# Gates, projections and merge of a hybrid decoder block, by token instead of by feature

## The chip, the cores and the metric

The kernel runs on one core of a Trainium2 chip. The metric is the device time of one execution in microseconds (us); the median of several runs is compared. All times below come from those runs or from one profiled execution of the kernel before.

## The reference, cut to what matters

256 tokens, model width 2048, float32. The change touches the gated merge of two token mixers:

```python
u = rms_norm(h, g_mix)
proj = u @ w_in                       # (256, 8704)
q, k, v, z, gb, gc, gate_a, gate_c = jnp.split(proj, split_points, axis=-1)
...
y_attn = sliding_window_attention(q, k, v, attn_sinks) @ w_attn_proj     # K = 1024
y_conv = short_gated_conv(z, gb, gc, conv_w) @ w_conv_proj               # K = 1024
merged = sigmoid(gate_a) * y_attn + sigmoid(gate_c) * y_conv             # (256, 2048)
h = h + merged @ w_mix_out                                               # K = 2048
```

Cross attention to 256 memory tokens and a SwiGLU block follow, and are not changed.

## The kernel before, in words

**Products.** Every product takes its float32 weights from DRAM in tiles of 256 rows (two k of 128) by 512 columns (`weights`, L72). SP issues the load of `raw` (5 buffers). ScalarE (ACT) rounds it to `whi` (L57), VectorE (DVE) makes the rest `wlo` (L58); each of these has 3 buffers. The activations are kept as a high and a low part too. TensorE (PE) then has two forms of product:

- `gemm_ft` (L88) gives the result by feature: weights are the stationary operand, 128 features at a time, and four such groups fill four accumulators in PSUM (of 5). For each k and group it issues one matmul of 512 columns (`whi` against high and low activations side by side, L98) and one of 256 (`wlo` against the high part, L102): 8 matmuls for each k, 3072 columns. At the end each group costs an ACT copy of half the accumulator (L109) and what `evac` yields; the first step runs at once, the rest is put into `pending` and is taken up between the weight tiles of the next product (L78).
- `gemm_tf` (L114) gives it by token: the activations of 128 tokens are stationary, the 512 weight columns move. For each k and each of two token blocks it issues three matmuls of 512 columns (L124, L125, L126): 6 for each k, 3072 columns, in two accumulators. `evac` runs once for each token block.

**Order of the work.** One loop after another: q, k, v (`gemm_tf`), six conv products, then the gates (L544, 8 products of 16 k: four fill `sa`, four fill `sc`), then for each 512-column chunk c the attention projection (L593, 8 k) and the conv projection (L594, 8 k), then W_mix_out (L638, four products of 16 k that read the merged features `MG`). "Hooks" are small pieces of other work issued ahead of a given weight tile: attention during the gates, and during the projections (`mem_hooks`, L582) the loads, squares and turning of the memory tokens. A planner then writes each engine's queue: it simulates the program, takes the work traced first among what it believes ready, and so can move work ahead. `keep_in_program_order` (L216) keeps the first turning instruction of a pair behind what was traced before it on its engine; the second one is free to move. Each queue then runs strictly in its order.

**Around the change.** `evac_g` (L554) adds the halves, scales by the norm's factor and takes the sigmoid: two DVE and two ACT instructions for each group. `evac_a` (L566) multiplies the attention projection by its gate into `sa`; `evac_m` (L573) multiplies the conv projection by its gate, adds `sa` and splits the sum into `MG`: by feature is what W_mix_out needs as its stationary operand. Token-major data can be turned in two ways that exist here already: by a bounce through DRAM (`bounce_out` L235 writes `hd`, `bounce_in` L240 reads it back in four transfers, `feat` L207 turns 32x32 blocks on DVE with L214 and splits), as the SwiGLU stage does through POOL's queue (L819), or by TensorE transposes into PSUM (`h_turn`, L728).

Of the kernel before, what the change touches and what calls it, by code (L numbers as in the profile page):

```python
# [10 lines left out]
F32 = mybir.dt.float32  # L11
# [6 lines left out]
P = 128  # L18
D = 2048
# [22 lines left out]
def hybrid_block(ctx, tc, a, out):  # L42
# [220 lines left out]
    with ExitStack() as ph:  # L263
# [72 lines left out]

        sa = mp.tile([P, KD, T], F32, tag="sa", name="sa")


        def rotary(s_sb, nh):  # L340
            for t in range(NT):
              for h0 in range(0, nh, 8):
# [4 lines left out]
                sn = rope[:, t:t + 1, 1, :].broadcast_to([P, n8, HD // 2])  # L347
                tm = [sa[:, i, :].rearrange("p (h d) -> p h d", d=HD // 2)[:, :n8, :] for i in range(4)]
                tt = nc.gpsimd.tensor_tensor
# [155 lines left out]

        sc = mp.tile([P, KD, T], F32, tag="sc", name="sc")
        steps = {
# [36 lines left out]
        for dst, base in ((sa, AW + 2 * KVW + 3 * CW), (sc, AW + 2 * KVW + 3 * CW + D)):  # L544
            for c in range(D // C):
                hooks = {4 * j + 2: [f] for j, f in enumerate(steps.get(i, ()))}
                i += 1
                if i == 8:
                    mem_open()
                    do = mem_do  # L550
                    hooks = {0: [lambda: do["stage"](0)], 2: [lambda: do["stage"](1)],
                             4: [lambda: do["nat"](0)], 6: [lambda: do["nat"](1)]}

                def evac_g(m, p0, p1, c=c, dst=dst):  # L554
                    o = dst[:, c * (C // P) + m, :]
                    add(o, p0, p1)
                    yield
                    scale(o, r0[1])
                    nc.scalar.activation(o, o, AF.Sigmoid)

                gemm_ft(W, KD, X1, base + c * C, evac_g, hooks=hooks)


        MG = xp.tile([P, KD, 2, T], F32R, tag="X", name="MG")
        for c in range(D // C):
            def evac_a(m, p0, p1, c=c):  # L566
                mm = c * (C // P) + m
                s = sp.tile([P, T], F32, tag="s1", name="s1", bufs=4)
                add(s, p0, p1)
                yield  # L570
                nc.vector.tensor_tensor(out=sa[:, mm, :], in0=s, in1=sa[:, mm, :], op=ALU.mult)

            def evac_m(m, p0, p1, c=c):  # L573
                mm = c * (C // P) + m
                s = sp.tile([P, T], F32, tag="s1", name="s1", bufs=4)
                add(s, p0, p1)
                yield
                nc.vector.tensor_tensor(out=s, in0=s, in1=sc[:, mm, :], op=ALU.mult)
                nc.vector.tensor_tensor(out=s, in0=s, in1=sa[:, mm, :], op=ALU.add)
                split(MG[:, mm, 0, :], MG[:, mm, 1, :], s)  # L580

            def mem_hooks(g):  # L582
# [3 lines left out]
                if g < 4:  # L586
                    hk[2].append(lambda: do["turn"](g, 0))
                    hk[4].append(lambda: do["turn"](g, 2))
                    if g < 2:
                        hk[4].append(lambda: do["stage"](g + 2))  # L590
                return hk

            gemm_ft(rows_kp(a["w_attn_proj"][0]), AW // P, oT, c * C, evac_a, hooks=mem_hooks(2 * c))  # L593
            gemm_ft(rows_kp(a["w_conv_proj"][0]), KC, yc, c * C, evac_m, hooks=mem_hooks(2 * c + 1))  # L594
        while pending:
            next(pending.pop(0), None)
        ms.close()
# [16 lines left out]
    with ExitStack() as ph:  # L614
# [20 lines left out]
        def h_feat(c, k, g, X):  # L635
            feat(hs[c], C // P, k, 2, c * (C // P) + k, g, X)

        for c in range(D // C):  # L638
            hooks = {4: [lambda: nc.gpsimd.dma_start(h[:, :, c * C:(c + 1) * C], xv[:, :, c * C:(c + 1) * C])]}
            if c:  # L640
                hooks[4].append(lambda: h_stage(c - 1))
            if c == D // C - 1:
                hooks[4].append(mem_rms)
            gemm_tf(rows_kp(a["w_mix_out"][0]), KD, MG, c * C, residual(c, ss1), hooks=hooks)

# [213 lines left out]
```

## Time and profile before

| | |
|---|---|
| median of 3 runs | 1441.95 us (1441.08 to 1443.12) |
| profiled execution, its own time | 1436.75 us |
| its span, first to last instruction | 1434.9 us |
| TensorE busy | 1418.9 us (99%) |
| VectorE, ScalarE, GpSimd busy | 858.8, 691.1, 95.0 us |

How to read it: PE is TensorE's matmuls, PEld its weight loads, DVE VectorE, ACT ScalarE, POOL GpSimd, SP the queue of weight loads. L12 is line 12 of the kernel. A row of the timeline gives start, length, engine, line, operation, out<-in, shapes and count; in square brackets the idle time of the engine before it and what ended it. The lengths of neighbouring matmuls overlap, so rates are read from start to start. The profiled execution was 5.2 us shorter than the median; differences are worked out in it and carried to the median.

### The profile page before, as it was taken

What the parts mean: (1) busy time and instruction counts of PE and PEld (TensorE: products, weight loads), DVE (VectorE), ACT (ScalarE), POOL (GpSimd) and SP (SyncE); (2) the same over time, 40 slices, a digit from 0 to 9 for tenths busy, and PEclk for the clock granted to TensorE, in tenths of its full rate; (3) what the DMA queues carried; (4) which work ended last, traced back from release to release, by engine and by line L of the source; (5) the groups of instructions that cost most, each with busy time, mean ns of one, the idle gap of its engine ahead of it and who ended that gap; (6) DMA issues with size and microseconds to landing.
All of it is one profiled execution on the core that took longest, in us unless ns stands there. A gap on an engine that the chain in (4) does not pass through costs nothing.

```text
span 1434.9 us, 18603 instructions
## 1 busy us (share of the span) xinstructions
PE 1418.9 (99%) x7006; PEld 1190.6 (83%) x7006; DVE 858.8 (60%) x1162; ACT 691.1 (48%) x979; POOL 95.0 (7%) x145
## 2 busy tenths in 40 slices
PE   9999999999999999999999999999999999999997
PEld 7888888888888888899888888888888888888886
DVE  5458678565569865585655555555444455555554
ACT  6443545554456654466644444444333444434443
POOL 1081000010001010000000000000000000000000
PEclk9999999999999999999999999999999999999999
DMA  8665454476667677764667777767666677777663
GB/s 269 192 176 172 138 171 150 150 219 203 190 199 216 204 248 235 249 201 150 207 187 223 221 221 219 214 211 221 193 192 194 203 215 221 220 211 230 204 191 118
DMA packets 150186, 288.66 MB, mean 201 GB/s; under 512 B 10084, under 2 KB 18880, under 8 KB 149968
## 3 DMA queue, kind: packets, MB, share of 16 engines
q1 hardware_dynamic: 144192, 269.52, 61.7%
q0 software_dynamic: 5872, 17.94, 4.7%
q8 instruction: 55, 0.90, 0.3%
q14 instruction: 35, 0.29, 0.1%
q10 hardware_dynamic: 32, 0.01, 0.0%
HBM read 277.47 MB, written 9.96 MB: 200 GB/s over the span
## 4 chain that ended last, share of the span: by engine, by line
PE 95%; POOL 2%; DMA 1%; ACT 1%; issue 1%; DVE 0%; SPq 0%; ACTq 0%; POOLq 0%; DVEq 0%
PE acc L125 21%; PE acc L124 21%; PE acc L126 21%; PE acc L98 20%; PE acc L102 10%; PE sps L445 1%; PE ops L498 1%; PE tp L487 0%; POOL sa L351 0%; POOL sa L350 0%; DMA hd<-h 0%; DMA x<-in_x 0%; DMA hst<-hd 0%; POOL sa L353 0%; PE tp L733 0%
## 5 line engine op out<-in xcount | busy, mean ns | idle before, releaser
L58 DVE TENSOR_TENSOR wlo<-raw,whi 128x1024 fp32r<-128x1024 f32 (+1 forms) x506 | 607.8, 1206 | 501.9 <-ACT whi L57 501.6
L57 ACT CAST whi<-raw 128x1024 fp32r<-128x1024 f32 (+1 forms) x506 | 520.2, 1031 | 651.3 <-PE acc L126 448.1
L98 PE MATMUL acc<-X,whi 128*128 128x512 f32 x960 | 329.2, 397 | 0.0
L125 PE MATMUL acc<-wlo,X 128*128 128x512 f32 x800 | 311.2, 390 | 0.0
L126 PE MATMUL acc<-whi,X 128*128 128x512 f32 x800 | 310.5, 389 | 0.0
L124 PE MATMUL acc<-whi,X 128*128 128x512 f32 x800 | 280.2, 390 | 1.8 <-ACT X L227 1.8
L102 PE MATMUL acc<-X,wlo 128*128 128x256 f32 x960 | 247.8, 281 | 0.0
L98 PEld LDWEIGHTS acc<-X,whi 128*128 128x128 f32 x960 | 176.7, 188 | 35.2 <-issue 0.8
L102 PEld LDWEIGHTS acc<-X,wlo 128*128 128x128 f32 x960 | 180.7, 188 | 11.0 <-issue 0.8
L124 PEld LDWEIGHTS acc<-whi,X 128*128 128x128 f32 x800 | 149.8, 188 | 33.4 <-ACT X L227 2.6
L126 PEld LDWEIGHTS acc<-whi,X 128*128 128x128 f32 x800 | 150.1, 188 | 31.1
L125 PEld LDWEIGHTS acc<-wlo,X 128*128 128x128 f32 x800 | 150.2, 188 | 30.9
L125 PE MATMUL acc<-wlo,gT 128*128 128x512 f32 x352 | 137.0, 389 | 0.0
L126 PE MATMUL acc<-whi,gT 128*128 128x512 f32 x352 | 136.9, 389 | 0.0
L124 PE MATMUL acc<-whi,gT 128*128 128x512 f32 x352 | 123.1, 389 | 0.0
L125 PEld LDWEIGHTS acc<-wlo,gT 128*128 128x128 f32 x352 | 66.1, 188 | 14.0 <-DVE wlo L58 0.3
L124 PEld LDWEIGHTS acc<-whi,gT 128*128 128x128 f32 x352 | 66.1, 188 | 13.8
L126 PEld LDWEIGHTS acc<-whi,gT 128*128 128x128 f32 x352 | 66.1, 188 | 13.6
L125 PE MATMUL acc<-wlo,MG 128*128 128x512 f32 x128 | 49.9, 390 | 0.4 <-DVE wlo L58 0.4
L126 PE MATMUL acc<-whi,MG 128*128 128x512 f32 x128 | 49.8, 389 | 0.0
L214 DVE STREAM_TRANSPOSE xt<-sg 128x256 f32<-128x256 f32 x44 | 26.5, 623 | 32.3 <-DMA sg<-hd 32.3
L124 PE MATMUL acc<-whi,MG 128*128 128x512 f32 x128 | 44.9, 389 | 0.0
(195 smaller groups left out, 1183.0 us busy)
## 6 DMA issues: line engine op xcount, KB each, us to landing
raw<-in_w_ffn_in SPq DMA_DIRECT2D x176, 512.0 KB, 3.8
raw<-in_w_in SPq DMA_DIRECT2D x134, 512.0 KB, 4.0
raw<-in_w_ffn_out SPq DMA_DIRECT2D x88, 512.0 KB, 3.6
raw<-in_w_mix_out SPq DMA_DIRECT2D x32, 512.0 KB, 5.3
raw<-in_w_attn_proj SPq DMA_DIRECT2D x16, 512.0 KB, 5.1
raw<-in_w_conv_proj SPq DMA_DIRECT2D x16, 512.0 KB, 5.5
hd<-gu POOLq DMA_DIRECT2D x11, 512.0 KB, 4.4
sg<-hd POOLq DMA_DIRECT2D x44, 128.0 KB, 4.6
```

The source lines that it names most:

```text
L57: nc.scalar.copy(hi, src)
L58: nc.vector.tensor_tensor(out=lo, in0=src, in1=hi.bitcast(F32), op=ALU.subtract)
L98: nc.tensor.matmul(ps[m], lhsT=hi[:, k, ms], rhs=X[:, kk].rearrange("p s t -> p (s t)"), start=(kk == 0), stop=False,)
L102: nc.tensor.matmul(ps[m][:, :T], lhsT=lo[:, k, ms], rhs=X[:, kk, 0, :], start=False, stop=(kk == kt - 1),)
L124: nc.tensor.matmul(o, lhsT=xh, rhs=hi[:, k, :cols], start=(kk == 0), stop=False)
L125: nc.tensor.matmul(o, lhsT=xh, rhs=lo[:, k, :cols], start=False, stop=False)
L126: nc.tensor.matmul(o, lhsT=xl, rhs=hi[:, k, :cols], start=False, stop=(kk == kt - 1))
L214: i = nc.vector.transpose(xt[:, k, :].rearrange("p (j b) -> p j b", b=Q), v[:, k0 + k, j0:j0 + nj, :])
L445: nc.tensor.matmul(sps[par][:, j].rearrange("p a b -> p (a b)"), lhsT=qT[b:b + 64, hh // 2, t * P:(t + 1) * P], rhs=kT[b:b + 64, sw, kv // ...
L498: nc.tensor.matmul(ops[64 * par:64 * par + 64], lhsT=v_sb[:, kb, vs], rhs=pt[:, t + kb, par::2, :], start=(kb == 0), stop=(kb == t),)
```

## The change

Gates, both projections and the merge use `gemm_tf`. `sa` and `sc` are laid out by chunk and token. A gate leaves PSUM by one ACT instruction per token block, the merge works on 512 columns of 128 tokens. Each merged chunk has to be turned to features for W_mix_out: chunks 0 to 2 are written to DRAM on POOL's queue; 0 and 1 are read back at once into the chunk of `sc` that is free by then and turned by DVE during the attention projections two chunks later; 2 is read back into a buffer of the next stage's pool (`mg`) at the start of W_mix_out and turned during its first product; chunk 3 is turned by 16 TensorE transposes right behind the last projection. The rows of W_mix_out are taken in the order that this turning gives (`rows_pk`), in the same tiles.

```diff
@@ -334,7 +334,7 @@
 
         gemm_tf(W, KD, X1, AW, evac_kv)
 
-        sa = mp.tile([P, KD, T], F32, tag="sa", name="sa")
+        sa = mp.tile([P, D // C, NT, C], F32, tag="sa", name="sa")
 
 
         def rotary(s_sb, nh):
@@ -345,7 +345,7 @@
                 x1, x2 = v[:, :, 0, :], v[:, :, 1, :]
                 cs = rope[:, t:t + 1, 0, :].broadcast_to([P, n8, HD // 2])
                 sn = rope[:, t:t + 1, 1, :].broadcast_to([P, n8, HD // 2])
-                tm = [sa[:, i, :].rearrange("p (h d) -> p h d", d=HD // 2)[:, :n8, :] for i in range(4)]
+                tm = [sa[:, i // 2, 0, (i % 2) * T:(i % 2 + 1) * T].rearrange("p (h d) -> p h d", d=HD // 2)[:, :n8, :] for i in range(4)]
                 tt = nc.gpsimd.tensor_tensor
                 tt(out=tm[0], in0=x1, in1=cs, op=ALU.mult)
                 tt(out=tm[1], in0=x2, in1=sn, op=ALU.mult)
@@ -503,7 +503,7 @@
                 sl = slice(t * P, (t + 1) * P)
                 split(oT[:, 2 * g:2 * g + 2, 0, sl], oT[:, 2 * g:2 * g + 2, 1, sl], ops)
 
-        sc = mp.tile([P, KD, T], F32, tag="sc", name="sc")
+        sc = mp.tile([P, D // C, NT, C], F32, tag="sc", name="sc")
         steps = {
             0: [qk_T], 1: [lambda: scores(0)], 2: [lambda: probs_T(0), lambda: scores(1)],
             3: [lambda: values(0), lambda: probs_T(1), lambda: scores(2)],
@@ -551,33 +551,26 @@
                     hooks = {0: [lambda: do["stage"](0)], 2: [lambda: do["stage"](1)],
                              4: [lambda: do["nat"](0)], 6: [lambda: do["nat"](1)]}
 
-                def evac_g(m, p0, p1, c=c, dst=dst):
-                    o = dst[:, c * (C // P) + m, :]
-                    add(o, p0, p1)
-                    yield
-                    scale(o, r0[1])
-                    nc.scalar.activation(o, o, AF.Sigmoid)
-
-                gemm_ft(W, KD, X1, base + c * C, evac_g, hooks=hooks)
+                def evac_g(t, p, c=c, dst=dst):
+                    nc.scalar.activation(dst[:, c, t, :], p, AF.Sigmoid, scale=r0[0][:, t:t + 1])
+
+                gemm_tf(W, KD, X1, base + c * C, evac_g, hooks=hooks)
 
 
         MG = xp.tile([P, KD, 2, T], F32R, tag="X", name="MG")
+        NC4 = C // P
+
+        def mg_feat(c, k):
+            feat(sc[:, c].rearrange("p t (j f) -> p (t j) f", f=P), NC4, k, 2, c * NC4 + k, None, MG, late=True)
+
         for c in range(D // C):
-            def evac_a(m, p0, p1, c=c):
-                mm = c * (C // P) + m
-                s = sp.tile([P, T], F32, tag="s1", name="s1", bufs=4)
-                add(s, p0, p1)
-                yield
-                nc.vector.tensor_tensor(out=sa[:, mm, :], in0=s, in1=sa[:, mm, :], op=ALU.mult)
-
-            def evac_m(m, p0, p1, c=c):
-                mm = c * (C // P) + m
-                s = sp.tile([P, T], F32, tag="s1", name="s1", bufs=4)
-                add(s, p0, p1)
-                yield
-                nc.vector.tensor_tensor(out=s, in0=s, in1=sc[:, mm, :], op=ALU.mult)
-                nc.vector.tensor_tensor(out=s, in0=s, in1=sa[:, mm, :], op=ALU.add)
-                split(MG[:, mm, 0, :], MG[:, mm, 1, :], s)
+            def evac_a(t, p, c=c):
+                nc.vector.tensor_tensor(out=sa[:, c, t, :], in0=p, in1=sa[:, c, t, :], op=ALU.mult)
+
+            def evac_m(t, p, c=c):
+                o = sc[:, c, t, :]
+                nc.vector.tensor_tensor(out=o, in0=p, in1=o, op=ALU.mult)
+                nc.vector.tensor_tensor(out=sa[:, c, t, :], in0=o, in1=sa[:, c, t, :], op=ALU.add)
 
             def mem_hooks(g):
                 hk = {2: [lambda: do["sums"](g)], 4: []}
@@ -588,12 +581,24 @@
                     hk[4].append(lambda: do["turn"](g, 2))
                     if g < 2:
                         hk[4].append(lambda: do["stage"](g + 2))
+                if g in (4, 6):
+                    hk.setdefault(4, []).append(lambda: mg_feat(g // 2 - 2, 0))
+                    hk[6] = [lambda: mg_feat(g // 2 - 2, 2)]
                 return hk
 
-            gemm_ft(rows_kp(a["w_attn_proj"][0]), AW // P, oT, c * C, evac_a, hooks=mem_hooks(2 * c))
-            gemm_ft(rows_kp(a["w_conv_proj"][0]), KC, yc, c * C, evac_m, hooks=mem_hooks(2 * c + 1))
-        while pending:
-            next(pending.pop(0), None)
+            gemm_tf(rows_kp(a["w_attn_proj"][0]), AW // P, oT, c * C, evac_a, hooks=mem_hooks(2 * c))
+            gemm_tf(rows_kp(a["w_conv_proj"][0]), KC, yc, c * C, evac_m, hooks=mem_hooks(2 * c + 1))
+            if c < D // C - 1:
+                hd = bounce_out(sa[:, c], nc.gpsimd)
+            if c < D // C - 2:
+                bounce_in(hd, sc[:, c].rearrange("p t (j f) -> p (t j) f", f=P), nc.gpsimd)
+        for k in range(0, NC4, 2):
+            tp = tps.tile([P, 2, T], F32, tag="tp", name="tp")
+            for i in range(2):
+                for t in range(NT):
+                    nc.tensor.transpose(tp[:, i, t * P:(t + 1) * P], sa[:, D // C - 1, t, k + i::NC4], ident)
+            kk = KD - NC4 + k
+            split(MG[:, kk:kk + 2, 0, :], MG[:, kk:kk + 2, 1, :], tp)
         ms.close()
 
     def residual(c, ss, r=None):
@@ -635,13 +640,26 @@
         def h_feat(c, k, g, X):
             feat(hs[c], C // P, k, 2, c * (C // P) + k, g, X)
 
+        mg = []
+
+        def mg_in():
+            mg.append(cp.tile([P, NJ, P], F32, tag="hst", name="mg", bufs=4))
+            bounce_in(hd, mg[0], nc.gpsimd)
+
+        def mg_last(k):
+            feat(mg[0], NC4, k, 2, (D // C - 2) * NC4 + k, None, MG, late=True)
+
         for c in range(D // C):
             hooks = {4: [lambda: nc.gpsimd.dma_start(h[:, :, c * C:(c + 1) * C], xv[:, :, c * C:(c + 1) * C])]}
             if c:
                 hooks[4].append(lambda: h_stage(c - 1))
             if c == D // C - 1:
                 hooks[4].append(mem_rms)
-            gemm_tf(rows_kp(a["w_mix_out"][0]), KD, MG, c * C, residual(c, ss1), hooks=hooks)
+            if not c:
+                hooks[0] = [mg_in]
+                hooks.update({2: [lambda: mg_last(0)]})
+                hooks[4].append(lambda: mg_last(2))
+            gemm_tf(rows_pk(a["w_mix_out"][0], NC4), KD, MG, c * C, residual(c, ss1), hooks=hooks)
 
         xkT = cp.tile([P, XH, T], F32, tag="xkT", name="xkT")
         xs = cp.tile([P, NJ * C], F32, tag="xs", name="xs")
```

## Rows read from the trace of the kernel before

**Rows 1.** The page: busy time of TensorE, and the chain that ended last by engine.
```profile
PE 1418.9 (99%) x7006; PEld 1190.6 (83%) x7006; DVE 858.8 (60%) x1162; ACT 691.1 (48%) x979; POOL 95.0 (7%) x145
...
PE 95%; POOL 2%; DMA 1%; ACT 1%; issue 1%; DVE 0%; SPq 0%; ACTq 0%; POOLq 0%; DVEq 0%
```
**Rows 2.** Timeline of TensorE, by feature: in the gates, and in the cross attention's W_xq.
```profile
399.99 0.40 PE L98 MATMUL acc<-X,whi 128*128 128x512 f32 x1
400.22 0.28 PE L102 MATMUL acc<-X,wlo 128*128 128x256 f32 x1
400.34 0.39 PE L98 MATMUL acc<-X,whi 128*128 128x512 f32 x1
...
650.02 0.39 PE L98 MATMUL acc<-X,whi 128*128 128x512 f32 x1
...
650.37 0.39 PE L98 MATMUL acc<-X,whi 128*128 128x512 f32 x1
```
**Rows 3.** Timeline of TensorE, by token, in the SwiGLU stage.
```profile
710.67 0.39 PE L125 MATMUL acc<-wlo,X 128*128 128x512 f32 x1
710.89 0.39 PE L126 MATMUL acc<-whi,X 128*128 128x512 f32 x1
```
**Rows 4.** The chain in order of time: the same point of two successive gate products.
```profile
364.27 0.92 PE acc L98 x4
...
386.55 0.92 PE acc L98 x4
```
**Rows 5.** Timeline of VectorE: the same point of the SwiGLU stage, two products apart.
```profile
794.12 1.28 DVE L811 TENSOR_TENSOR gu<-acc,st 128x512 f32<-128x512 f32 x2
...
837.64 1.28 DVE L811 TENSOR_TENSOR gu<-acc,st 128x512 f32<-128x512 f32 x2
```
**Rows 6.** The projections' matmuls by tile: ns least/median/most, first and last start.
```profile
L98 PE MATMUL acc<-oT,whi x128: 387/396/496, 425.4 to 505.8; 128*128 128x512 f32 x128
...
L102 PE MATMUL acc<-yc,wlo x128: 274/281/385, 436.8 to 517.5; 128*128 128x256 f32 x128
```
**Rows 7.** Projection stage, windows: busy PE, PEld, DVE, ACT, POOL; clock, DMA share, GB/s.
```profile
425.00:472.00 47.00, 45.98 (x259) 39.36 (x258) 44.84 (x86) 32.24 (x62) 6.95 (x12) 1.00 0.75 214
472.00:518.00 46.00, 46.00 (x265) 40.23 (x264) 36.89 (x73) 27.38 (x49) 1.28 (x2) 1.00 0.65 207
```
**Rows 8.** Groups of instructions by shape: the add of two halves on VectorE.
```profile
L143 DVE TENSOR_TENSOR s<-acc,half 128x256 f32<-128x256 f32 x40 | 15.8, 418 | 1.6 <-ACT half L109 1.6
```
**Rows 9.** Timeline of TensorE: four transposes between matmuls at the start of SwiGLU.
```profile
704.87 0.63 PE L733 MATMUL tp<-ident,h 128*128 128x128 f32 x4
705.26 0.72 PE L124 MATMUL acc<-whi,X 128*128 128x512 f32 x2
705.82 0.63 PE L733 MATMUL tp<-ident,h 128*128 128x128 f32 x4
```
**Rows 10.** Timeline of POOL and VectorE: one bounce of a chunk in the SwiGLU stage.
```profile
795.70 0.72 POOL L237 DMA_DIRECT2D hd<-gu  x1 [36.38 <-DVE gu L811]
...
800.67 2.33 POOL L233 DMA_DIRECT2D sg<-hd  x4 [4.25 <-DMA hd<-gu]
...
808.54 0.64 DVE L214 STREAM_TRANSPOSE xt<-sg 128x256 f32<-128x256 f32 x1 [3.45 <-DMA sg<-hd]
```
**Rows 11.** VectorE's waits: total, times, longest; and W_mix_out's idle TensorE by line.
```profile
DVE xt L214 <- DMA sg<-hd: 32.3, 11, 3.5
...
DVE xt L214 <- DMA hst<-hd: 3.3, 1, 3.3
...
L125 PE MATMUL acc<-wlo,MG 128*128 128x512 f32 x128 | 49.9, 390 | 0.4 <-DVE wlo L58 0.4
```
**Rows 12.** Timeline of ScalarE: the rounding of one weight tile, by token.
```profile
802.78 1.05 ACT L57 CAST whi<-raw 128x1024 fp32r<-128x1024 f32 x1 [1.67 <-PE acc L126]
```
**Rows 13.** POOL's loads of h after the projections: timeline, and the DMA view.
```profile
523.53 2.93 POOL L639 DMA_DIRECT2D h<-in_x  x4 [19.05 <-PE acc L126]
...
h<-in_x POOLq DMA_DIRECT2D x4, 512.0 KB, 8.0
```

## The prediction

> **What bounds the kernel now.** I read the page first. TensorE is busy for 99% of the span and the chain that ended last lies on it for 95% [rows 1]; no other engine is near that. So a change is worth what it takes off TensorE's queue, plus or minus the waits it makes there, and work that only leaves DVE, ACT or POOL is worth nothing by itself.
>
> Busy time does not tell the rate, because neighbouring matmuls overlap. So I went to the timeline and read start to start. By feature, a 512-column matmul is followed after 0.23 us and its 256-column partner after 0.12 us: the pair takes 0.35 us, in the gates as well as in W_xq much later, with other neighbours [rows 2]. By token, a 512-column matmul takes 0.22 to 0.23 us [rows 3]. Both forms stream 3072 columns for each k: four pairs, or six single matmuls. Four pairs are 1.40 us, six singles about 1.36 us; the timeline's hundredths are too coarse for that difference, so I took whole products. Two successive gate products stand 386.55 − 364.27 = 22.28 us apart [rows 4], for 16 k: 1.3925 us each. In SwiGLU two products by token take 837.64 − 794.12 = 43.52 us [rows 5], for 32 k: 1.360 us each. The clock is at its full level in the projections [rows 7], as in the rest of the span, so it gives or takes nothing.
>
> The projections are a little worse than their form explains. They run from 425.4 us to the start of the last conv matmul at 517.5 us [rows 6], with one W_mix_out matmul of 0.23 us slipped in between and the last matmul's own 0.12 us behind: 517.5 + 0.12 − 0.23 − 425.4 = 92.0 us for 8 products of 8 k, where 64 x 1.3925 would be 89.1. The windows show why: up to 472 us DVE is busy for 44.84 of 47 us and TensorE loses a microsecond; behind that DVE eases to 36.89 of 46 [rows 7].
>
> **The change, part by part.**
>
> Gates, 8 products of 16 k: 128 x (1.3925 − 1.360) = **−4.2 us**. All of it is TensorE's queue.
>
> Projections: 64 x 1.360 = 87.0 instead of 92.0: **−5.0 us**, of which 64 x 0.0325 = 2.1 is the form and 2.9 the stalls and rough edges.
>
> Whether those 2.9 go is a question of DVE. Per chunk, before, it does 8 operations of 128x256 for the attention projection and 16 for the conv projection, each like the add of 0.42 us [rows 8]: 24 x 0.42 = 10.1 us. After, it does 6 operations of 128x512 from PSUM or SBUF, 1.28 us for two [rows 5]: 3.8 us. For the two chunks that lie beside the memory turning this is 12.6 us less, 32 of the 43.5 us that the stretch would last, so the overload goes. The last two chunks get the turning of chunks 0 and 1 instead, each four block transposes of 0.64 us [rows 10] and two subtractions of about 0.64, the same 3.8 us: still below the present load. ACT loses the copies of halves and has fewer, wider sigmoids and splits. None of this costs TensorE anything while DVE keeps ahead. PSUM helps: two accumulators per product instead of four of five.
>
> What is new there is a wait. The planner lets the second transposing instruction of a pair go ahead, to where it believes the data has landed; in SwiGLU it then stood in DVE's queue for 3.45 us with weight remainders behind it, 11 waits of about 3 us in all [rows 10, 11]. There TensorE did not feel it: ACT rounds a tile when TensorE frees a buffer [rows 12], two tiles of 2 x 1.36 = 2.72 us before it is needed, so 5.44 − 1.05 (rounding) − 1.2 (remainder) = 3.2 us are in hand. In the projections DVE has other work at the same time. Bounds: 0 (as in SwiGLU) and 3.45 us (one wait in full); nearer to SwiGLU, since the load falls: **+0.8 us**.
>
> TensorE transposes of chunk 3: 16, in four groups. In the group shown four transposes start at 704.87 and the next matmul at 705.26, 0.39 us; the two matmuls behind take 0.56 us to the next group instead of 0.45 [rows 9]. So 0.5 us a group: **+2.0 us**. Nothing hides it.
>
> The seam into W_mix_out, which no row shows. Let E be the end of the last projection matmul. W_mix_out can run its first 8 k from chunks 0 and 1, 10.9 us, plus the 2.0 us of transposes: chunk 2 must be split at E + 12.9, chunk 3 at 5.4 us later. Chunk 3 is no issue: four DVE operations, two of them behind E, then transposes and a split. The transposes come early in TensorE's queue and may wait for DVE by a fraction of a microsecond. Chunk 2 is close. Its buffer lies where the old pool was, so the read-back waits on POOL for the old tiles' last use. If that is the last merge operation only, it is E + 1.5 to 2.7 us (one weight remainder in between). If it is the whole old pool, transposes included, about E + 4.5; the loads of h that wait for the same release today left POOL at 523.53, 6 us behind the last projection matmul [rows 13]. From the first read-back issue to the first transposing instruction is 808.54 − 800.67 = 7.9 us [rows 10]; two transposes and the rounding add 1.9. So chunk 2 is ready between E + 11.3 and E + 15.8, later by another 1.2 if all four transposes go first: a wait of 0 to 4.1. The same delay stands in DVE's queue, where 3.2 us are covered; the nearest case, a wait of 3.3 us for `hst` in W_mix_out today, cost TensorE 0.4 us [rows 11]. Together 0 to 4.5, I take **+1.5 us**. The Trainium skill, DMA: Bandwidth & Descriptors, "Anatomy of one DMA — SWDGE (gpsimd) path", gives about 2.0 us fixed plus bytes at 436 GB/s for a transfer; by it the read-back would take 2.33 (four issues) + 2.3 = 4.6 us, the seam would cost nothing and the sum be −6.4. The row's 7.9 us is what I use.
>
> At nothing: the write-backs and read-backs of chunks 0 and 1 on POOL. POOL is busy 1.28 of 46 us [rows 7]; the bounce lasts 13 us [rows 10] and the memory loads queued behind it are used two projections, 22 us, later; if that cover failed, ACT's squares and with them the rounding would wait. The write of chunk 2 has a whole pair of projections. The loads of h are queued behind the read-back and move by its 2.33 us of issue [rows 10]; h is added at the end of a 22 us product. W_mix_out's tiles are as large as before, from other rows. SP's queue is passed by nothing.
>
> Sum: −4.2 − 5.0 + 0.8 + 2.0 + 1.5 = **−4.9 us**. Against the profiled execution that is 1436.75 − 4.9 = 1431.85; the median stood 5.2 higher, so I forecast 1441.95 − 4.9 = **1437.0 us**.
>
> **The rivals.**
>
> *Columns alone set the rate.* If TensorE is paid by columns, and the 0.0325 us per k belongs to the stage and not to the form, the 192 k give back 6.3 us: −4.9 + 6.3 = +1.4, 1443.4 us, no measurable change. Against it: the pair takes 0.35 us in two stages with different neighbours [rows 2]. For it: I compare different stages. The Trainium skill, TensorE: Matmul & The Clock Gate, "Back-to-back issue gap", has a warm gap of N/2.4 plus about 2.5 ns, so that two matmuls less per k save 5 ns, 1.0 us here, and the sum would be +0.4. The rows disagree with it: a product by token comes to 1360 / 6 = 227 ns a matmul, not 216, so a matmul costs more here than its columns.
>
> *Waits at their upper bounds.* 3.45 in the projections and 4.5 at the seam: −9.2 + 2.0 + 8.0 = +0.8, and anything above −2.9 counts as no change: 1439 to 1443. For it: both waits were found on DVE in the trace; against it: both were nearly free there [rows 11].
>
> *Slower: POOL takes the loads of h first.* Both sets wait for the same release, and before, the planner sent all four loads of h in one go [rows 13]. If they go ahead of the read-back of chunk 2, that is issued 2.9 us later and lands among four transfers that need 8.0 us each: E + 4.5 + 2.9 + 7.9 + 4 (half of those 8.0, my guess for what they take from each other) + 1.9 = E + 21, 8 us late instead of 1.5. DVE's queue holds the next weight remainders behind it. −4.9 + 6.6 = +1.7 at that point, and if the second pair's splits and remainders queue too (3 to 4 us), 1447 us. It decides from a seam of about 9.3 us (−6.4 + 9.3 = +2.9). Against it: the read-back is traced first.
>
> **How the numbers follow.** The forecast with its sizes about right: 0.65. Columns alone: 0.06. Waits at their bounds: 0.20. POOL's order: 0.09. A run of this kernel can be told from no change at about 0.2%, 2.9 us: below 1439.1 is faster, above 1444.8 slower. The forecast alone is faster, the next two are the same, the last is slower. Own range of the forecast: both waits at 0 and 0.4 us of today's idle gone give −7.6, and the measurement adds about 1 (the runs of before span 1441.08 to 1443.12): 1433 to 1439. With the waits at their bounds it reaches 1442.5; what lies above is left out.
>
> **What would show it.** In the profile after: gate products 21.8 us apart, the projections near 87 us; no matmul by feature between the conv products and W_xkv; 16 transposes in one place of about 2 us; DVE below 80% in the projections; a wait of TensorE for chunk 2 or for a weight remainder of 0 to 4 us in the first W_mix_out product. I am wrong if the gates keep 22.3 us, if TensorE waits over 5 us at the seam, or if POOL issues h ahead of `mg`.

## The result and the profile after

The kernel after takes 1449.32 us (median of 4 runs, 1444.93 to 1450.47), the kernel before, run beside it, 1441.51 us (4 runs, 1439.37 to 1443.12): ratio 1.0056, interval 1.0038 to 1.0073. It is slower by about 8 us. The forecast was 1437.0 us, with 1442.5 as the upper end of its range.

Which stage lost it is read from the starts of the first matmul of each stage. The profiled executions are 1436.75 us before and 1450.47 us after.

| stretch, us | before | after | difference |
|---|---|---|---|
| up to the first conv matmul | 78.3 | 80.4 | +2.1 |
| conv products and gates | 347.1 | 343.9 | −3.2 |
| projections and first W_mix_out product | 113.8 | 127.0 | +13.2 |
| the other three W_mix_out products | 65.9 | 65.3 | −0.7 |
| cross attention to the first product on `gT` | 363.3 | 364.9 | +1.6 |
| first to last product on `gT` | 446.2 | 447.4 | +1.2 |

The change touches the second and third stretch: −3.2 + 13.2 = +10.0 us. The others are not its work: in another profile of the kernel before (run `before_again`, 1440.14 us) the first and the fifth stretch were 79.8 and 364.0 us, the second and third 347.0 and 113.8 as here. So outside the change the first profile of before was lucky, by about 2 us. The medians differ by 7.8 us, 2 less than the two stretches; the runs of after themselves spread over 5.5 us.

First comes the page of the kernel after, as in [rows 1]. TensorE is busy for 2 us more than before although it issues 376 matmuls less.

```profile
PE 1420.9 (98%) x6630; PEld 1175.6 (81%) x6630; DVE 831.1 (57%) x1046; ACT 670.1 (46%) x891; POOL 104.2 (7%) x160
```

Next come the waits of the kernel after (in total, times, longest, in us), the counterpart of [rows 11].

```profile
DVE xt L214 <- DMA sg<-hd: 43.7, 11, 5.2
...
POOL mg L233 <- PE tp L599: 18.6, 1, 18.6
...
DVE xt L214 <- DMA sc<-hd: 13.4, 2, 7.3
...
PE acc L124 <- ACT MG L57: 7.1, 1, 7.1
...
PE acc L125 <- DVE wlo L58: 5.6, 5, 2.6
...
DVE xt L214 <- DMA mg<-hd: 4.8, 1, 4.8
```

The fourth line is the largest part of the loss: TensorE stood for 7.1 us in one piece, for a part of `MG`. The third and most of the fifth belong together: DVE stood twice in front of a block transpose of a read-back chunk, and TensorE ran out of weight remainders there for 4.0 of the 5.6 us (the rest is in SwiGLU).

The timeline of TensorE in the kernel after says where this is. The last projection matmul starts at 517.87, W_mix_out at 518.11.

```profile
380.77 0.62 PE L124 MATMUL acc<-whi,X 128*128 128x512 f32 x2
...
402.53 0.62 PE L124 MATMUL acc<-whi,X 128*128 128x512 f32 x2
...
424.30 0.64 PE L124 MATMUL acc<-whi,oT 128*128 128x512 f32 x2
...
496.16 0.50 PE L125 MATMUL acc<-wlo,oT 128*128 128x512 f32 x1 [2.56 <-DVE wlo L58]
...
506.95 0.63 PE L124 MATMUL acc<-whi,yc 128*128 128x512 f32 x2
...
518.11 0.62 PE L124 MATMUL acc<-whi,MG 128*128 128x512 f32 x2
...
524.35 0.89 PE L599 MATMUL tp<-ident,sa 128*128 128x128 f32 x6
...
530.10 0.27 PE L254 MATMUL tp<-ident,rw 128*128 128x128 f32 x1
...
537.50 0.79 PE L124 MATMUL acc<-whi,MG 128*128 128x512 f32 x1 [7.12 <-ACT MG L57]
538.09 0.63 PE L125 MATMUL acc<-wlo,MG 128*128 128x512 f32 x1
538.51 0.63 PE L124 MATMUL acc<-whi,MG 128*128 128x512 f32 x1
...
542.74 0.54 PE L126 MATMUL acc<-whi,MG 128*128 128x512 f32 x1
543.12 0.40 PE L124 MATMUL acc<-whi,MG 128*128 128x512 f32 x1
543.36 0.39 PE L125 MATMUL acc<-wlo,MG 128*128 128x512 f32 x1
```

There are three readings. The gate product takes 402.53 − 380.77 = 21.76 us, as forecast against [rows 4]. The last conv projection takes 518.11 − 506.95 = 11.16 us for 48 matmuls, 232.5 ns each, where the gate's 96 take 226.7: the projections don't run at the rate of the other products by token. And behind the wait the matmuls stand 0.42 us apart or more, until 543.12.

The queues of POOL, DVE and ACT in the kernel after show how the wait came about.

```profile
452.42 0.74 POOL L237 DMA_DIRECT2D hd<-sa  x1 [8.60 <-DVE sa L573]
...
457.90 2.33 POOL L233 DMA_DIRECT2D sc<-hd  x4 [2.92 <-DMA hd<-sa]
...
469.21 0.64 DVE L214 STREAM_TRANSPOSE xt<-sc 128x256 f32<-128x256 f32 x1 [6.11 <-DMA sc<-hd]
...
494.37 0.63 DVE L214 STREAM_TRANSPOSE xt<-sc 128x256 f32<-128x256 f32 x1 [7.26 <-DMA sc<-hd]
...
525.53 2.35 POOL L233 DMA_DIRECT2D mg<-hd  x4 [18.64 <-PE tp L599]
527.87 2.85 POOL L653 DMA_DIRECT2D h<-in_x  x4
...
535.66 2.17 DVE L214 STREAM_TRANSPOSE xt<-mg 128x256 f32<-128x256 f32 x4 [4.82 <-DMA mg<-hd]
...
536.83 0.62 ACT L57 CAST MG<-xt 128x512 fp32r<-128x512 f32 x1 [5.48 <-DVE xt L214]
```

The read-back of chunk 2 leaves POOL at 525.53, and what POOL waited for is the last transpose of chunk 3 on TensorE. The planner had put those transposes two weight tiles into W_mix_out (the row of 524.35 above), so the old pool was released late; the first block transpose of its data started 10.1 us after its issue. Behind two block transposes came the first rounding, and this part of chunk 2 was ready at 537.5. TensorE had run out of other work at 530.4. Before, the loads of h waited for such a release too [rows 13], but nothing needed them soon.

Last come the windows of the kernel after: the first two as in [rows 7], the last two the wait and the time behind it (busy PE, PEld, DVE, ACT, POOL; clock, DMA share, GB/s).

```profile
424.00:472.00 48.00, 46.53 (x200) 37.43 (x200) 37.10 (x54) 26.49 (x40) 10.03 (x17) 1.00 0.85 240
472.00:518.00 46.00, 43.44 (x187) 34.90 (x187) 32.93 (x45) 19.91 (x25) 5.07 (x8) 1.00 0.77 233
...
530.00:538.00 8.00, 0.88 (x4) 0.51 (x3) 2.77 (x6) 1.80 (x3) 0.72 (x2) 0.68 1.03 308
538.00:545.00 7.00, 6.98 (x21) 5.00 (x20) 2.69 (x4) 1.53 (x2) 0.00 (x0) 0.64 0.41 135
```

DVE did fall below 80% in the projections (37.10 of 48, 32.93 of 46), and TensorE idles there all the same, 1.5 and 2.6 us: busy time was not what decided. In the last two rows the granted clock is 0.68 and 0.64, which mixes its two levels: it fell during the wait, is 0.50 from 533.0 to 543.0, and so behind the wait TensorE runs at the lower one, 1.2 GHz, for a while.

### The profile page after: what moved, and what is told of

Read it like the earlier page. It is cut to its first block, busy times and chain, and to the rows that moved or that the text cites. A ratio compares the mean times of both kernels' runs of the same rounds, so it can differ in the third digit from the quotient of the medians.

```text
span 1448.7 us, 17648 instructions
## 1 busy us (share of the span) xinstructions
PE 1420.9 (98%) x6630; PEld 1175.6 (81%) x6630; DVE 831.1 (57%) x1046; ACT 670.1 (46%) x891; POOL 104.2 (7%) x160
## 5 line engine op out<-in xcount | busy, mean ns | idle before, releaser
L125 PE MATMUL acc<-wlo,X 128*128 128x512 f32 x1056 | 412.5, 391 | 1.0 <-DVE wlo L58 1.0
L126 PE MATMUL acc<-whi,X 128*128 128x512 f32 x1056 | 410.8, 390 | 0.0
L124 PE MATMUL acc<-whi,X 128*128 128x512 f32 x1056 | 371.4, 391 | 2.6 <-ACT X L227 2.6
L125 PEld LDWEIGHTS acc<-wlo,X 128*128 128x128 f32 x1056 | 198.5, 188 | 45.1 <-DVE wlo L58 2.6
L124 PEld LDWEIGHTS acc<-whi,X 128*128 128x128 f32 x1056 | 197.9, 188 | 44.5 <-ACT X L227 3.0
L126 PEld LDWEIGHTS acc<-whi,X 128*128 128x128 f32 x1056 | 198.5, 188 | 40.7
L98 PE MATMUL acc<-X,whi 128*128 128x512 f32 x448 | 154.7, 398 | 0.0
L102 PE MATMUL acc<-X,wlo 128*128 128x256 f32 x448 | 116.4, 283 | 0.0
L98 PEld LDWEIGHTS acc<-X,whi 128*128 128x128 f32 x448 | 82.5, 188 | 16.4 <-issue 0.8
L102 PEld LDWEIGHTS acc<-X,wlo 128*128 128x128 f32 x448 | 84.4, 189 | 5.8 <-DVE wlo L58 0.7
```

The lines of the kernel that those rows point to most:

```text
L98: nc.tensor.matmul(ps[m], lhsT=hi[:, k, ms], rhs=X[:, kk].rearrange("p s t -> p (s t)"), start=(kk == 0), stop=False,)
L102: nc.tensor.matmul(ps[m][:, :T], lhsT=lo[:, k, ms], rhs=X[:, kk, 0, :], start=False, stop=(kk == kt - 1),)
L124: nc.tensor.matmul(o, lhsT=xh, rhs=hi[:, k, :cols], start=(kk == 0), stop=False)
L125: nc.tensor.matmul(o, lhsT=xh, rhs=lo[:, k, :cols], start=False, stop=False)
L126: nc.tensor.matmul(o, lhsT=xl, rhs=hi[:, k, :cols], start=False, stop=(kk == kt - 1))
```

## The experiments

Two theories of the loss stand after this: **the seam** (the read-back is issued too late, and the wait brings a slower clock behind it) and **the waits of DVE** in the projections. A third thing is open, **the rate** of 232 ns. The rival to all of it is chance in other stages. Each kernel is the kernel after with the edit shown, unless it says otherwise. The timed variants stand in one table. The stage times are from the start of the first matmul on `oT`, on `MG` and of the second W_mix_out product, in the profiled execution; ratios are to the runs of before on the same chip. The rows come from several chips, so ratios are to be compared, not medians.

| run | conv, gates | projections | first W_mix_out | median us (runs) | ratio to before |
|---|---|---|---|---|---|
| before (first profile) | 347.1 | 90.1* | 23.7* | 1441.51 (4) | 1 |
| after | 343.9 | 93.8 | 33.2 | 1449.32 (4) | 1.0056 (1.0038 to 1.0073) |
| e1_chunk2_tensor | 343.9 | 92.9 | 23.1 | 1442.50 (10) | 1.0025 (1.0013 to 1.0036) |
| e2_early_readback | 343.8 | 91.0 | 23.0 | 1438.81 (10) | 0.9991 (0.9981 to 1.0002) |
| e3_fill | 343.9 | 92.7 | 31.1 | 1449.04 (4) | 1.0064 (1.0043 to 1.0084) |
| e4_pin_both | 343.8 | 89.2 | 31.7 | 1443.31 (7) | 1.0023 (1.0012 to 1.0034) |
| e6_gates_only | 343.8 | 90.0* | 23.7* | 1437.92 (11) | 0.9983 (0.9973 to 0.9993) |
| e7_early_and_pinned | 343.9 | 89.2 | 23.0 | 1434.85 (5) | 0.9956 (0.9942 to 0.9970) |
| e9_pinned_all | 343.8 | 89.2 | 23.0 | 1433.32 (5) | 0.9956 (0.9942 to 0.9969) |
| e10_tensor_pinned | 343.8 | 90.2 | 23.1 | 1439.10 (11) | 0.9992 (0.9983 to 1.0001) |
| e11_before_pinned | 348.5** | 90.1* | 23.7* | 1439.64 (11) | 0.9990 (0.9981 to 0.9999) |

(*) In these three one W_mix_out matmul starts ahead of the last projection matmuls; the projections proper are 1.9 us longer than shown and the product as much shorter. (**) In this profile the granted clock was 0.89 from 100 to 115 us, in the conv products, where the first profile of before has 1.00.

**Chunk 2 by TensorE too.** Its turning becomes eight transposes behind its own conv projection, so no read-back stands at the seam.

```diff
+        def mg_turn(c):
+            for k in range(0, NC4, 2):
...
+                        nc.tensor.transpose(tp[:, i, t * P:(t + 1) * P], sa[:, c, t, k + i::NC4], ident)
...
-            if c < D // C - 1:
+            if c >= D // C - 2:
+                mg_turn(c)
+            else:
                 hd = bounce_out(sa[:, c], nc.gpsimd)
-            if c < D // C - 2:
```

> Chunk 2 is turned by TensorE too, so nothing is read back at the seam. Theory (TensorE waits there for the read-back of chunk 2, 7.1 us, and then runs some 5.5 us at half clock): the first W_mix_out product takes about 22.5 us instead of 33.2, 8 more transposes cost about 1.0 us, and the time falls by about 9.5 us, to about 1440. Rival (the seam is slow for another reason, such as W_mix_out's rows in the new order or the loads of h): the product stays above 28 us and the time within 4 us of the changed kernel.

The seam wait is gone and the first W_mix_out product is 10.1 us shorter, while the projections are still at 92.9 us: their waits are another thing. The profiled execution is 9.6 us below that of the kernel after (1440.82), but the ratio fell by 0.3% only, about 4.5 us; the runs go from 1440.82 to 1447.41, so the profile is the fastest of them, and where the others lose the rest it does not show.

**Chunk 2 read back early.** The read-back goes out as soon as the chunk is written, into one of the memory tokens' staging buffers, which are free by then; the pool of these buffers is closed behind the first W_mix_out product instead of ahead of it. Its turning comes two weight tiles later and is pinned in the program's order.

```diff
+            if c == D // C - 2:
+                mem_do["mg"] = mem_do["tmp"].tile([P, NJ, P], F32, tag="mst", name="mg")
+                bounce_in(hd, mem_do["mg"], nc.gpsimd)
...
-            mg.append(cp.tile([P, NJ, P], F32, tag="hst", name="mg", bufs=4))
-            bounce_in(hd, mg[0], nc.gpsimd)
+            mg.append(mem_do["mg"])
...
-                hooks.update({2: [lambda: mg_last(0)]})
-                hooks[4].append(lambda: mg_last(2))
+                hooks[4].append(lambda: mg_last(0))
+                hooks[6] = [lambda: mg_last(2)]
```

> Chunk 2 is still bounced through DRAM, but is read back right behind its write into a buffer of the memory staging, which does not lie in the closed pool. Theory (what is late is the release of the old pool, not the transfer): no wait of TensorE for chunk 2, the clock stays up, the first W_mix_out product takes about 22.5 us and the time falls by about 9 us. Rival (the read-back itself, about 10 us to the last landing, or VectorE's turning is too slow wherever it stands): a wait of over 3 us stays.

The timeline of POOL in this run shows that the read-back leaves 20 us earlier. The loads of h, whose buffer lies where the old pool was, still wait for TensorE's transposes; so it is the release of that pool that holds things back. That wait costs nothing here.

```profile
505.58 2.35 POOL L233 DMA_DIRECT2D mg<-hd  x4 [1.76 <-DMA hd<-sa]
525.33 2.85 POOL L653 DMA_DIRECT2D h<-in_x  x4 [17.40 <-PE tp L602]
```

The first W_mix_out product takes 23.0 us instead of 33.2 and the ratio falls from 1.0056 to 0.9991, about 9 us, as the seam theory has it. TensorE has the same work as in the kernel after; what changed is where `mg` lies, when it is read back, and where it is turned. The later turning can't be what helped: in the kernel after, the data came at 535.66 and TensorE needed them from 530.4.

**Fill the wait.** TensorE gets 30 matmuls that nobody reads, ahead of the ones that wait. This adds work; it tells what of the 10 us is the clock.

```diff
+        def fill():
+            fp_ = tps.tile([P, C], F32, tag="tp", name="fill")
+            for j in range(30):
+                i = nc.tensor.matmul(fp_, lhsT=MG[:, 0, 0, :P], rhs=MG[:, 0].rearrange("p s t -> p (s t)"),
+                                     start=(j == 0), stop=(j == 29))
+                if not j:
+                    tc.keep_in_program_order(i)
...
+                hooks[8] = [fill]
```

> The changed kernel with 30 matmuls of 512 columns (6.8 us at 227 ns), whose result is not used, placed in TensorE's queue where it waits for chunk 2. Theory (the wait also costs by the lower clock behind it, about 2.5 to 3 us): the granted clock stays at its full level through the seam and the time falls by about 2.5 us although there is more work. Rival (the slow matmuls behind the wait are slow for their data, not for the clock): no change or up to 1 us slower.

The timeline of TensorE and the same two windows in this run:

```profile
528.62 6.96 PE L652 MATMUL fill<-MG 128*128 128x512 f32 x30
...
537.71 0.50 PE L126 MATMUL acc<-whi,MG 128*128 128x512 f32 x1 [0.68 <-DVE MG L58]
```

```profile
530.00:538.00 8.00, 7.29 (x32) 5.54 (x31) 4.24 (x7) 1.24 (x2) 0.00 (x0) 1.00 0.98 315
538.00:545.00 7.00, 7.00 (x32) 5.76 (x32) 3.04 (x4) 2.10 (x2) 0.00 (x0) 1.00 0.48 156
```

The clock stays at 1.00, and the product is 33.2 − 31.1 = 2.1 us shorter though TensorE is held for 6.96 + 0.68 us instead of 7.12. So the slow matmuls behind the wait cost 2.1 + 0.5 = 2.6 us. The count in the kernel after gives 2.9: from 537.50 to 543.12, 12 matmuls take 5.62 us where 12 x 0.227 = 2.72 would do. The expected fall of the time did not come: the median shows no gain against the kernel after (4 runs over 6 us), and in the profile the last two stretches of the first table, which the edit does not touch, are 0.5 and 2.4 us longer. So this rests on the stretch alone.

**Pin both transposes.** The second block transpose of a pair keeps its place in the program's order too.

```diff
-            if late and not k:
+            if late and (not k or late == 2):
...
-            feat(sc[:, c].rearrange("p t (j f) -> p (t j) f", f=P), NC4, k, 2, c * NC4 + k, None, MG, late=True)
+            feat(sc[:, c].rearrange("p t (j f) -> p (t j) f", f=P), NC4, k, 2, c * NC4 + k, None, MG, late=2)
```

> For chunks 0 and 1 both transposing instructions of each pair keep their place, not only the first. Theory (the free one stands in VectorE's queue 6 to 7 us for its data, with weight remainders behind it, and TensorE loses 1.6 and 2.7 us): both waits go, the projections take about 89.5 us instead of 93.8 and the time falls by about 4 us. Rival (VectorE has too much to do there, wherever the instructions stand): waits of the same total turn up at other places and the time stays within 1 us.

Two of the waits in this run:

```profile
PE acc L124 <- ACT MG L57: 6.5, 1, 6.5
...
DVE xt L214 <- DMA sc<-hd: 0.4, 1, 0.4
```

DVE's waits for `sc` shrink to 0.4 us and the projections to 89.2 us, 4.6 less; the seam wait stays (6.5 us). The ratio falls from 1.0056 to 1.0023. Both theories hold, each with its own part. What the free transposes cost varies from profile to profile: without this edit the projections took 93.8, 92.9, 91.0 and 92.7 us (after, e1, e2, e3), 1.8 to 4.6 more than with it.

**Both mends together.**

> Chunk 2 read back early and every transposing instruction of the merge pinned, together. Theory (the two causes add): the projections take 89.2 us as with the pins alone, the first W_mix_out product about 23 us as with the early read-back alone, no wait of TensorE over 0.5 us between the gates and W_mix_out; about 1.7 us below the early read-back alone, that is some 3 us (0.2%) below the kernel before. Rival (with one wait gone the other work is late instead): the projections stay at 91 us and the time is that of the kernel before.

The ratio is 0.9956: this kernel is faster than the one before, by about 6 us, more than the 3 expected. The stage times of the two mends stand side by side in it, 89.2 and 23.0.

**The rate.** First, other stationary operands in the same stage: on e7, one attention projection reads `XM` in place of `oT` and one conv projection `MG` in place of `yc`. Then e7 with `yc` filled with zeros ahead of the last conv projection.

```diff
-            gemm_tf(rows_kp(a["w_attn_proj"][0]), AW // P, oT, c * C, evac_a, hooks=mem_hooks(2 * c))
-            gemm_tf(rows_kp(a["w_conv_proj"][0]), KC, yc, c * C, evac_m, hooks=mem_hooks(2 * c + 1))
+            gemm_tf(rows_kp(a["w_attn_proj"][0]), AW // P, do["XM"][:, 0:KC] if c == 2 else oT, c * C, evac_a, hooks=mem_hooks(2 * c))
+            gemm_tf(rows_kp(a["w_conv_proj"][0]), KC, MG[:, 0:KC] if c == 3 else yc, c * C, evac_m, hooks=mem_hooks(2 * c + 1))
```

```diff
             gemm_tf(rows_kp(a["w_attn_proj"][0]), AW // P, oT, c * C, evac_a, hooks=mem_hooks(2 * c))
+            if c == 3:
+                nc.gpsimd.memset(yc.bitcast(F32), 0.0)
```

> As e7, but the attention projection of chunk 2 takes the normed memory tokens XM as its stationary operand instead of oT, and the conv projection of chunk 3 takes the first half of MG instead of yc, so the output leaves out these two products' own inputs. Theory (the stationary operand's tile sets the rate: oT and yc cost 232 ns a matmul, MG 227 ns everywhere in W_mix_out): the last conv projection falls to 227 ns a matmul, 10.9 us instead of 11.15. Rival (it is the stage: its weights, its other engines, its transfers): it stays at 232 ns with MG too.

> As e7, but yc is filled with zeros by POOL before the last conv projection, which leaves out that projection's input. If the 232 ns a matmul come with the place of oT and yc in the memory, the last conv projection stays at 232 ns; if they come with the values in them, it changes, to 227 ns or below.

The same piece of the last conv projection in TensorE's timeline, first with `MG`, then with zeros in `yc`:

```profile
503.50 0.40 PE L126 MATMUL acc<-whi,MG 128*128 128x512 f32 x1
...
510.08 0.39 PE L126 MATMUL acc<-whi,MG 128*128 128x512 f32 x1
```

```profile
504.17 0.39 PE L126 MATMUL acc<-whi,yc 128*128 128x512 f32 x1
...
514.39 0.40 PE L126 MATMUL acc<-whi,yc 128*128 128x512 f32 x1
```

The first pair stands 29 matmuls apart, 6.58 us: 226.9 ns. With `XM`, in the attention projection of the same run, a matmul takes 226.7 ns (32 of them in 7.25 us). The second pair stands 44 apart, 10.22 us: 232.3 ns. The stage and its traffic are the same; the values of `yc` were changed and made no difference (those of `oT` were not changed). So it is something of the tiles `oT` and `yc` themselves. No run moved them, so what it is stays open.

The kernel before has it too, with these tiles moving. Two rows of its timeline, 64 matmuls apart with no wait between them, are one projection product of 8 k: 506.32 − 495.09 = 11.23 us, where half of a gate product on `X` is 11.14 [rows 4].

```profile
495.09 0.40 PE L98 MATMUL acc<-oT,whi 128*128 128x512 f32 x1
...
506.32 0.40 PE L98 MATMUL acc<-yc,whi 128*128 128x512 f32 x1
```

The runs of e5 and e8 took 1435.72 and 1435.80 us, one run each.

**The gates alone.** This is the kernel before with gates by token and everything else as it was.

```diff
-                def evac_g(m, p0, p1, c=c, dst=dst):
...
-                gemm_ft(W, KD, X1, base + c * C, evac_g, hooks=hooks)
+                def evac_g(t, p, c=c, dst=dst):
+                    o = dst[:, c * (C // P) + 2 * t:c * (C // P) + 2 * t + 2, :].rearrange("p m t -> p (m t)")
+                    nc.scalar.activation(o, p, AF.Sigmoid, scale=r0[0][:, t:t + 1])
+
+                gemm_tf(W, KD, X1, base + c * C, evac_g, hooks=hooks)
```

> The kernel before with only the gates by token; the projections and the merge stay by feature and take the gates in the wrong places, so the merge is computed from other gate values. Theory (a product of 16 k takes 21.76 us by token and 22.28 by feature): conv products and gates together take 343 us instead of 347.1, and the time falls by 4 us (0.28%). Rival (columns alone set the rate, the gain comes from elsewhere): 347 us and no change.

> The kernel before, unchanged, profiled once more, since its profiled execution was 3 to 5 us below its median and the changed kernels' were near theirs. If the 1.9 us that all changed kernels show before the conv products, and the 1.5 us in cross attention and the first SwiGLU part, are chance, this profile has them too (start of the conv products at about 80.2 us instead of 78.3); if they come with the change, it is at 78.3 us again.

The stretch is 3.2 us shorter, as in the kernel after, and the median 2.5 us (0.17%). That is less than the 4 us expected. The last five gate products have the forecast period, 21.76 us for 22.29. The missing 1 us of the 4.2 lies in the first three, beside the attention's pieces: together they take 76.6 us by token, in e6 and in the kernel after, and 77.0 by feature, a gain of 0.4 where 1.6 was forecast. Why stays open.

**SwiGLU's transposes.** Turning `gT` there has the same free second transpose, in the kernel before as well [rows 11], and in the profile of the kernel after its waits were longer. e9 is e7 with both pinned there too; e11 is the kernel before with that alone; e10 is e1 with the pins of e4.

```diff
-                feat(sgs[c], NC4, k, 2, (c - b0) * NC4 + k, None, gT, late=True)
+                feat(sgs[c], NC4, k, 2, (c - b0) * NC4 + k, None, gT, late=2)
```

> As e7, and in the SwiGLU stage too every transposing instruction keeps its place. Theory (the free ones there wait for their data for 3 to 5 us, which TensorE feels by chance, 0.3 to 1.2 us at a time): no wait of TensorE for weight remainders in SwiGLU, VectorE's 11 waits for the bounced chunks gone, the time 1 to 2 us below e7, about 1433.5 us. Rival (those waits are nearly all covered): the same time as e7 within 0.5 us.

> The kernel before with the SwiGLU pins of e9 alone, to see how much of e9's gain is the change's. Theory (by feature the projections have no free transposing instruction of the merge, so only SwiGLU's waits go, 1.4 us in the second profile of the kernel before): about 1 to 1.5 us faster, ratio 0.999, and e9 stays about 5 us below it. Rival (the pins are most of e9's gain): 4 us faster or more.

> Chunk 2 turned by TensorE, chunks 0 and 1 bounced with every transposing instruction pinned. Theory (the two causes add here too, and 8 transposes cost 1.0 us): the projections take about 90.2 us and the time comes out about 1 us above e7, some 1436 us, below the kernel before by 0.3%. Rival (the wait of 1.7 us seen in the projections with chunk 2 turned by TensorE comes from TensorE's own transposes waiting for VectorE, not from the bounce): that wait stays and the time is 2.5 us or more above e7.

The waits in e7, then e9:

```profile
DVE xt L214 <- DMA sg<-hd: 40.6, 11, 5.0
...
PE acc L125 <- DVE wlo L58: 0.9, 3, 0.5
```

```profile
DVE xt L214 <- DMA sg<-hd: 3.5, 1, 3.5
...
PE acc L125 <- DVE wlo L58: 0.3, 1, 0.3
```

37 us of DVE's waits go, and TensorE gains little: its waits for remainders fall by 0.6 us, and the median by 1.5 us (on another chip), as expected, but the ratio not at all. So DVE's waits were nearly all covered, as the prediction read them in SwiGLU. e9 has the lowest median, 1433.32 us, and e11 shows that the pins alone are worth 0.1% (ratio 0.9990, 0.9981 to 0.9999); the rest of its gain is the mended change. e10 is a half miss. Its projections do as expected, and its first product too, but it stays 4 us behind e7; in its profile DVE's waits in SwiGLU are 46.7 us with one of 6.0, and TensorE waits there 4.7 us for remainders. So the rival's wait in the projections is gone, and the time came out as the rival had it. e1, which turns chunk 2 in the same way, has 46.0 us of these waits, and eleven runs of e10 at 1437.66 to 1441.09 say that it is not one execution's chance. Why this version meets them more often stays open; e10 with SwiGLU's transposes pinned, which could settle it, was not run.

## Why the prediction was wrong

The direction was wrong, and the seam made it so: without its wait (e2) the kernel is level with the one before. Point by point:

- **Gates, −4.2.** The product's period came as worked out, 21.76 us for 21.8. The stretch gave 3.2, because the first three products gained 1.1 less than worked out.
- **Projections, −5.0.** The form was to give 2.1 and the stalls of before 2.9. With the waits mended the projections take 89.2 us, 92.0 − 89.2 = 2.8 less. 64 x 1.360 = 87.0 carried the rate of SwiGLU [rows 5] to other stationary tiles; with `oT` and `yc` a matmul takes 232.4 ns, 64 x 6 x 0.2324 = 89.2. The form by feature was slower on these tiles too than the 89.1 that the gates' rate gave. An undisturbed product took 11.23 us (the rows of the kernel before under "The rate"), 89.8 for all eight, where by token it takes 11.16. So the form gave 0.6 of the 2.8 instead of 2.1, and the stalls of before were 2.2 and not 2.9. "Columns alone set the rate" came nearly true for this stage alone, by another mechanism.
- **Waits in the projections, +0.8.** Too small. The free second transpose stood for 6.11 and 7.26 us, not 3.45, TensorE idled for 1.5 and 2.6 us by the windows, and the projections are 4.6 us longer than with both pinned (e4). The upper bound was taken from SwiGLU, where the bounce lasts 13 us; here it took 469.2 − 452.4 = 16.8 us from the write to the waiting transpose, beside traffic of 240 GB/s instead of the 214 there was before. The mechanism was right, and the cover was larger than the 3.2 us worked out (6.11 − 1.5 = 4.6, 7.26 − 2.6 = 4.7); the length of the waits was off.
- **Transposes, +2.0.** I counted 16; the chunk of 512 columns is 4 blocks for each of 2 token blocks, so 8. They take about 1 us, from 524.0 to 525.0. e7's first product is 1.2 us longer than before (23.0 against 113.8 − 92.0 = 21.8).
- **The seam, +1.5.** This is the step that decided. It is the rival "waits at their upper bounds" in kind, but with bounds too low. I saw the release of the whole old pool as the later case and put it at E + 4.5, at most at E + 6 (15.8 = 6 + 7.9 + 1.9), with the transposes right behind the last projection. The planner put them two weight tiles later, so the read-back was issued at 525.53, E + 7.4. To the first block transpose it took 10.1 us instead of 7.9; why is open. Two block transposes and the rounding then took 1.8, as priced, and the other two, which I had added for the worst case, did not come ahead. Chunk 2 was ready at E + 19.4, and TensorE came to it at E + 12.3. That is 7.1 us of wait against a bound of 4.1, or 4.5 with DVE's part. And I had said that the clock gives or takes nothing: it fell during the wait and took 2.6 to 2.9 us more. In all, the first product is 10.2 us longer than in e2 and e7, which have the same work without the wait.
- **"POOL takes the loads of h first"** did not happen: the read-back of `mg` is issued ahead of h in the timeline. The rival named the right place and got near the size, and its reason was wrong.

The Trainium skill, DMA: Bandwidth & Descriptors, "Anatomy of one DMA — SWDGE (gpsimd) path", led to an estimate of 4.6 us for this read-back. The trace has 10.1 us from first issue to the first block transpose. The measurement decides: the page's figure is for one transfer, and it was no price for these four among others.

Mended, the change is worth what the forecast asked for: e7's stages give −3.2 − 2.8 + 1.2 = −4.8 us, and its ratio 0.9956 is −6.3 us, −4.3 to −8.4. That the sum agrees with the −4.9 on record is luck: the gates gave 1.0 us less and the projections' rate 2.2 less, and against that stand the waits that were mended away (0.8 and 1.5) and the transposes that were counted twice. As to the range, its upper end is 1441.95 + 0.8 = 1442.7 by its own sum, not 1442.5; the result lies above either.

## What to carry to other kernels

When a buffer lies in a space that another stage releases, date the release from where the planner or scheduler puts its last reader, and not from where the program text has it; a read-back that something needs soon belongs in a buffer that is free already. A wait of several microseconds on TensorE should be priced with the slower matmuls behind it. When a rate is carried from one product to another, check it with the same stationary operand, or at least say that it is another.

## What the runs showed of the hardware

- **Rate by tile.** In long streams of the same form, 512 columns at full clock, products took 226.7 to 226.9 ns a matmul with `X`, `XM` and `MG` stationary and 232.3 to 232.5 ns with `oT` and `yc`. Neither the stage (e5) nor, for `yc`, the values (e8) explain it. By feature, with these tiles moving, the difference was smaller: 11.23 us a product against 11.14.
- **The clock behind a wait.** In a wait of 7.1 us without matmuls the granted clock fell: it was 0.68 in the stretch of the wait and 0.64 in the next, and matmuls stood mostly 0.42 to 0.43 us apart until 543.12, 5.6 us behind the wait's end. The Trainium skill, TensorE: Matmul & The Clock Gate, "Back-to-back issue gap", has N / 1.2 ns as the gap of the slow level, by which an estimate for 512 columns is 427 ns; the trace agrees with 0.42 to 0.43 us.
- **Chance in SwiGLU.** The same waits there came to 32.3 us [rows 11] and 37.2 us in two profiles of the kernel before, and to 39.0 to 49.0 us in the variants that leave the stage as it was; TensorE's waits for remainders there go from none to 4.7 us. Of the edits only the pinned order removes them.
